# A two-layer gated-DeltaNet and sliding-window decoder trunk: the buffers, the places and the applied product of the adaLN modulation

## The chip, the cores and the metric

The kernel runs on one core of one Trainium2 chip. The metric is the device time of one execution in microseconds (us); of the kernel before, three runs have a median of 2365.28 us (2364.86 to 2368.85).

## The reference

All arithmetic is float32. Sequence length is 256, model width 2048, two layers. What matters here:

```python
c_act = silu(c)
for l in range(2):
    mod = c_act @ ada_w[l] + ada_b[l]                  # 2048 -> 3 x 2048
    shift, scale, gate = split(mod, 3)
    h = rmsnorm(x, norm_w[l]) * (1 + scale) + shift
    u = h @ w_in[l]                                    # q,k,v,beta,a,z_A | q,k,v,z_B | g_A,g_B
    o_a = gated_delta_rule(conv_silu(q, k, v), beta, a) -> per-head rmsnorm * silu(z_A)
    o_b = sliding_window_attention(rope(q), rope(k), v, sinks) * silu(z_B)
    y = sigmoid(g_A) * (o_a @ proj_a) + sigmoid(g_B) * (o_b @ proj_b)
    x = x + gate * (y @ w_out)
x = rmsnorm(x, final_norm_w)
```

`mod` is one vector of 6144 numbers per layer; its matrix `ada_w` holds 2048 x 6144 floats per layer and is read once.

## The kernel before, in words

**Layout.** Everything is kept transposed: features on the 128 partitions, the 256 tokens in the free dimension. A projection is cut into *tiles* of 128 output features. One tile needs a weight block of 128 x 2048 floats, which comes as two *halves* of 128 x 1024 (512 KB each).

**Products in two parts.** Each weight half is split into a high part and a remainder, so that TensorE's faster float32r products keep the precision: `load_half` (line 196) loads it into a buffer `win`, ScalarE casts it into `whi` (line 201) and VectorE subtracts to give `wlo` (line 202). The buffers are rings: five `win`, four `whi`, three `wlo` (line 31). The moving operand `h` is split the same way. `proj` (line 292) runs 16 k-steps per tile, each of two matmuls: `whi` with both parts of `h` (512 columns, line 289) and `wlo` with the high part (256 columns, line 290).

**Order of the work.** `_plan` (line 46) lists the tiles of a layer. Layer 0 begins with 32 gate tiles computed together while the modulation for layer 0 is made (`group_first`); layer 1 begins with a group of 8 (`group_next`). Then come, in both layers, `ba`, `kb`, `vb` (5 tiles); twice the batch `qa`, `ka`, `va` (8 tiles each) and `qb`/`zb` (16 tiles together); `za` (16); `pa` (16, in layer 1 with 8 gate tiles between); `pb` (16, in layer 1 with 16 gate tiles between); `wo` (16). The main loop (lines 965 to 999) takes them one by one: it loads the weights of the tile two ahead, emits the matmuls, advances the background work (the DeltaNet chain of a batch runs in pieces, one per tile, among the tiles that follow), calls the tile's handler, which evacuates the result, and may then emit modulation work. The tile framework turns this program order into one static order per engine; engines then wait for each other by semaphores, each one strictly in its order. All transfers are issued from SyncE's queue (SP), also in a fixed order.

**Background work of note.** `gdn_k` (line 589) inverts 32 x 32 triangles by 62 small VectorE operations (lines 644 to 653), sends the result through DRAM (`ydr`, `xdr`, lines 658 to 670) and TensorE then multiplies it (`T1p`, line 679). This falls into the `qb`/`zb` stage of each batch.

**Modulation.** The vectors for layer 0's shift and scale are made at the start (`ada_start`). The other 64 blocks (gate of layer 0; scale, shift, gate of layer 1) are made among the tiles: `ada_job` (line 171) makes one block of 128 values out of two halves of 128 x 1024. Each half is loaded into a buffer *of the weights' ring* (tag `win`, line 166) and at once multiplied and summed by one VectorE instruction (line 168); after the second, one or two tiny instructions (lines 177, 180) finish the block. A table `ADA_RATE` (line 28) says how many blocks each kind of tile is due; when the sum reaches one, a whole block, so two halves one behind the other, is emitted after the tile's handler (lines 991 to 994). By the start of `wo` in layer 0, 48 blocks must be there, and what is missing is emitted at once (line 977).

**The end of a layer.** `h_wo` (line 926) adds the gated product to x (lines 934, 935), squares it for the norm, and, in layer 0, writes the new x to DRAM (line 940), multiplies it *in place* by the next layer's scale (line 941) and makes the two float32r parts of the product (lines 949, 950) for the group of 8 gate tiles. `h_step` (line 376) later multiplies the scaled x by the row's reciprocal root to make `h`.

Of the kernel before, what the change touches and what calls it, by code (L numbers as in the profile page):

```python
# [11 lines left out]
F32 = mybir.dt.float32  # L12
F32R = mybir.dt.float32r
I32 = mybir.dt.int32
AF = mybir.ActivationFunctionType
ALU = mybir.AluOpType
# [3 lines left out]
P = 128  # L20
D = 2048
S = 256
KT = 16
# [1 line left out]
NH = 16  # L25
HB = 8
NB = NH // HB
ADA_RATE = [dict(qa=0.45, ka=0.45, va=0.0, qb=0.275, zb=0.275, za=0.54, pa=0.54, pb=0.54), dict(ga=0.3, pa=0.3, gb=0.3, pb=0.3)]
GRP = [32, 8]
SEG = [(0, 0, 4), (1, 0, 8), (0, 4, 12), (1, 8, 16), (0, 12, 16)]  # L30
NWIN, NWHI, NWLO = 5, 4, 3
BIG = 1.0e30
EPS = 1e-6

# [83 lines left out]
def build(nc):  # L118
# [11 lines left out]
    with ExitStack() as ctx:  # L130
# [3 lines left out]
        wp = pool("wp", 3)  # L134
        b8 = pool("b8", 1)
        sm = pool("sm", 2)
# [25 lines left out]

        modc = const.tile([P, L, 3, KT], F32, name="modc")

        def ada_half(l, part, ct, hf, acc):
            t = wp.tile([P, 1024], F32, name="adaw", tag="win", bufs=NWIN)
            dma(t, ada_d[l, part, ct, :, hf * 1024:(hf + 1) * 1024])
            V.scalar_tensor_tensor(t, t, 1.0, cact[:, hf * 1024:(hf + 1) * 1024], op0=ALU.mult, op1=ALU.mult,  # L168
                                   accum_out=acc[:, hf:hf + 1])

        def ada_job(l, part, ct):
            acc = sm.tile([P, 2], F32, name="modr", tag="modr", bufs=4)
            for hf in range(2):
                ada_half(l, part, ct, hf, acc)
            m = modc[:, l, part, ct:ct + 1]
            b = par[l][:, PC_ADAB + part * KT + ct:PC_ADAB + part * KT + ct + 1]
            V.tensor_scalar(m, acc[:, 0:1], acc[:, 1:2], b, op0=ALU.add, op1=ALU.add)
            if part == 1:
                nw = par[l][:, PC_NW + ct:PC_NW + ct + 1]
                V.tensor_scalar(m, m, 1.0, nw, op0=ALU.add, op1=ALU.mult)  # L180
# [194 lines left out]

        def h_step(l, k, xa, rstd, dst):
            t = sm.tile([P, S], F32, name="hn", tag="tA", bufs=3)
            V.tensor_tensor(t, xa, rstd, op=ALU.mult)
            sh = modc[:, l, 0, k:k + 1]
            A.activation(dst[:, 0:S], t, AF.Identity, bias=sh)  # L380
            V.scalar_tensor_tensor(dst[:, S:2 * S], t, sh, dst[:, 0:S].bitcast(F32), op0=ALU.add, op1=ALU.subtract)
# [39 lines left out]
        dma(par[1], par_d[1])  # L421
        rope_tables()
        ada_todo = [(0, 2, k) for k in range(KT)] + [(1, p_, k) for p_ in (1, 0, 2) for k in range(KT)]

        for l in range(L):
            pr = par[l]
# [499 lines left out]
            def h_wo(ps, i):  # L926
                nonlocal nacc, nlast
                if i % 8 == 0:
                    xnext[i // 8] = big("x", [P, 8, S], ("GT", "Y")[i // 8])
                xo = xnext[i // 8][:, i % 8, :]  # L930
                xr = sm.tile([P, S], F32, name="xr", tag="tB", bufs=2)
                dma(xr, x_d[i] if l == 0 else prev_x[i])
                gt = modc[:, l, 2, i:i + 1]
                V.scalar_tensor_tensor(xr, ps[:, S:2 * S], gt, xr, op0=ALU.mult, op1=ALU.add)
                V.scalar_tensor_tensor(xo, ps[:, 0:S], gt, xr, op0=ALU.mult, op1=ALU.add)
                if i == 0:
                    nacc = sm.tile([P, S], F32, name="nacc", tag="cv", bufs=2)
                nlast = norm_acc(nacc, xo, i)
                if l < L - 1:
                    dma(xs_dram[i], xo)  # L940
                    V.tensor_scalar(xo, xo, modc[:, l + 1, 1, i:i + 1], None, op0=ALU.mult)
                    n = S + 2
                    if i % 4 == 0:
                        raw.append(big("raw", [P, 4, 2 * n], ("QKT", "ek", "oT", "oT")[i // 4], F32R))
                        sh = modc[:, l + 1, 0, i:i + 4].unsqueeze(2).broadcast_to([P, 4, 2])
                        A.copy(raw[-1][:, :, S:n], sh)
                        V.tensor_tensor(raw[-1][:, :, n + S:2 * n], sh, raw[-1][:, :, S:n].bitcast(F32), op=ALU.subtract)
                    r = raw[-1][:, i % 4, :]
                    A.copy(r[:, 0:S], xo)
                    V.tensor_tensor(r[:, n:n + S], xo, r[:, 0:S].bitcast(F32), op=ALU.subtract)  # L950
                else:
                    V.tensor_scalar(xo, xo, pr[:, PC_FNW + i:PC_FNW + i + 1], None, op0=ALU.mult)

# [11 lines left out]
            for n in range(GRP[l], NT):  # L965
# [5 lines left out]
                for a in range(n, n + AHEAD + 1):  # L971
# [2 lines left out]
                            load_w(l, a)  # L974
                    elif l < L - 1 and (l + 1, a - NT) not in gtiles:
                        load_g(l + 1, a - NT)
                while what == "wo" and l == 0 and len(ada_todo) > KT:
                    ada_job(*ada_todo.pop(0))
                mov = {"pa": oA_hl, "pb": oB_hl, "wo": y_hl}.get(what, h)
                pg = proj(l, n, mov)  # L980
                ps = next(pg)
# [5 lines left out]
                if r is not None:  # L987
                    w = next(r, "end")
                    if w != "end":
                        streams.append([r, w or 0])  # L990
                acc_ada += ADA_RATE[l].get(what, 0.0)
                while ada_todo and acc_ada >= 1.0:
                    ada_job(*ada_todo.pop(0))
                    acc_ada -= 1.0
                if what == "za" and i % HB == HB - 1:
                    split_oA(i // HB)
# [85 lines left out]
```

## Time and profile before

| what | value |
|---|---|
| median of the three timed runs | 2365.28 us |
| the profiled execution, its own time | 2367.93 us |
| its span, first to last instruction | 2366.1 us |
| granted TensorE clock, mean | 0.989 |
| TensorE busy | 2292.6 us |
| VectorE busy | 1787.0 us |
| ScalarE busy | 1371.2 us |
| modulation instruction of line 168 | 128 times, 1221 ns in the mean |
| remainder of a weight half, line 202 | 724 times, 1220 ns in the mean |

In the rows of the profile PE is TensorE, PEld its weight loads, DVE is VectorE, ACT is ScalarE, SP is SyncE, which issues the transfers; `L202` is line 202 of the kernel. A row of the view by stretches gives, for a stretch of time in us from the start of the span: its length, then for each engine the busy time and in brackets the number of instructions, then the granted TensorE clock as a share of full speed, the share of the DMA engines' time in use, and GB/s. A row of the waits gives who waited for whom: the sum in us, how often, the longest. Matmuls overlap in the pipeline, so busy time of TensorE is not work at its peak.

### The profile page before, as it was taken

What the parts mean: (1) busy time and instruction counts of PE and PEld (TensorE: products, weight loads), DVE (VectorE), ACT (ScalarE), POOL (GpSimd) and SP (SyncE); (2) the same over time, 40 slices, a digit from 0 to 9 for tenths busy, and PEclk for the clock granted to TensorE, in tenths of its full rate; (3) what the DMA queues carried; (4) which work ended last, traced back from release to release, by engine and by line L of the source; (5) the groups of instructions that cost most, each with busy time, mean ns of one, the idle gap of its engine ahead of it and who ended that gap; (6) DMA issues with size and microseconds to landing.
All of it is one profiled execution on the core that took longest, in us unless ns stands there. A gap on an engine that the chain in (4) does not pass through costs nothing.

```text
span 2366.1 us, 39958 instructions
## 1 busy us (share of the span) xinstructions
PE 2292.6 (97%) x15094; PEld 2026.3 (86%) x15094; DVE 1787.0 (76%) x3160; ACT 1371.2 (58%) x2605; POOL 13.9 (1%) x20
## 2 busy tenths in 40 slices
PE   7999999899999998999999999999999999999997
PEld 6999888788887887888889888898888888888886
DVE  7997887866889677788676778757785567677766
ACT  4436556667666664444455665777667755444442
POOL 0000000000000000000000000000000000000000
PEclk9999999999999999999999999999999999999999
DMA  9998675656766567898766555635555467777764
GB/s 365 364 359 283 235 245 186 193 177 204 246 199 211 171 221 264 295 318 292 232 204 199 195 181 183 187 121 197 191 167 167 140 205 265 243 243 253 243 203 142
DMA packets 185603, 531.75 MB, mean 225 GB/s; under 512 B 40449, under 2 KB 69697, under 8 KB 179905
## 3 DMA queue, kind: packets, MB, share of 16 engines
q1 hardware_dynamic: 185410, 529.20, 66.9%
q8 instruction: 118, 1.93, 0.3%
q14 instruction: 75, 0.61, 0.1%
HBM read 512.26 MB, written 16.88 MB: 224 GB/s over the span
## 4 chain that ended last, share of the span: by engine, by line
PE 75%; DVE 11%; DMA 9%; issue 3%; ACT 2%; SPq 0%; DVEq 0%; ACTq 0%
PE mm L289 38%; PE mm L290 20%; DVE wlo L202 4%; DMA adaw<-ada 4%; PE mmg L251 2%; PE mmg L249 2%; PE mmg L250 2%; DMA xs_dram<-x 1%; DVE adaw L168 1%; DMA win<-w 1%; DMA oBs<-ob_dram 1%; PE o L742 1%; DVE cv L526 1%; PE sc L844 1%; PE ptr L871 1%
## 5 line engine op out<-in xcount | busy, mean ns | idle before, releaser
L289 PE MATMUL mm<-h,whi 128*128 128x512 f32 x3616 | 1292.3, 398 | 0.0
L202 DVE TENSOR_TENSOR wlo<-win,whi 128x1024 fp32r<-128x1024 f32 x724 | 882.0, 1220 | 244.7 <-PE mm L290 131.0
L290 PE MATMUL mm<-h,wlo 128*128 128x256 f32 x3616 | 1025.4, 284 | 7.1 <-DVE wlo L202 7.1
L201 ACT CAST whi<-win 128x1024 fp32r<-128x1024 f32 x724 | 753.4, 1047 | 443.1 <-PE mm L289 227.5
L289 PEld LDWEIGHTS mm<-h,whi 128*128 128x128 f32 x3616 | 681.7, 189 | 157.4 <-issue 4.3
L290 PEld LDWEIGHTS mm<-h,wlo 128*128 128x128 f32 x3616 | 682.7, 189 | 10.6 <-DVE wlo L202 10.2
L168 DVE SCALAR_TENSOR_TENSOR adaw<-adaw,cact 128x1024 f32<-128x1024 f32 x128 | 155.8, 1221 | 69.7 <-DMA adaw<-ada 69.4
L289 PE MATMUL mm<-oAhl,whi 128*128 128x512 f32 x512 | 184.4, 401 | 6.3 <-DVE oAhl L322 4.2
L289 PE MATMUL mm<-yhl,whi 128*128 128x512 f32 x512 | 181.8, 397 | 3.1 <-DVE yhl L924 3.1
L289 PE MATMUL mm<-oBhl,whi 128*128 128x512 f32 x512 | 180.8, 396 | 0.0
L317 DVE TENSOR_TENSOR ub<-ub,mm 128x256 f32<-128x256 f32 x290 | 120.7, 416 | 68.9 <-ACT ub L316 68.2
L526 DVE SCALAR_TENSOR_TENSOR cv<-ub,par,cv 128x255 f32<-128x255 f32 (+2 forms) x288 | 138.1, 480 | 32.6 <-ACT cv L524 29.1
L290 PE MATMUL mm<-oAhl,wlo 128*128 128x256 f32 x512 | 146.1, 286 | 1.1 <-DVE wlo L202 1.1
L290 PE MATMUL mm<-yhl,wlo 128*128 128x256 f32 x512 | 145.6, 284 | 1.6 <-DVE wlo L202 1.4
L249 PE MATMUL mmg<-h,whi 128*128 128x256 f32 x512 | 139.8, 287 | 6.3 <-ACT h L373 6.1
L290 PE MATMUL mm<-oBhl,wlo 128*128 128x256 f32 x512 | 144.2, 282 | 0.0
L250 PE MATMUL mmg<-h,whi 128*128 128x256 f32 x512 | 142.5, 286 | 0.0
L251 PE MATMUL mmg<-h,wlo 128*128 128x256 f32 x512 | 135.7, 287 | 3.2 <-DVE wlo L202 3.2
L316 ACT COPY ub<-mm 128x256 f32<-128x256 f32 x290 | 107.2, 370 | 38.0 <-PE mm L290 37.9
L289 PEld LDWEIGHTS mm<-oAhl,whi 128*128 128x128 f32 x512 | 98.1, 192 | 29.9 <-DVE oAhl L322 4.5
L289 PEld LDWEIGHTS mm<-yhl,whi 128*128 128x128 f32 x512 | 96.8, 189 | 25.8 <-DVE yhl L924 3.4
L289 PEld LDWEIGHTS mm<-oBhl,whi 128*128 128x128 f32 x512 | 96.2, 188 | 22.9
(261 smaller groups left out, 2600.2 us busy)
## 6 DMA issues: line engine op xcount, KB each, us to landing
win<-w SPq DMA_DIRECT2D x724, 512.0 KB, 4.7
adaw<-ada SPq DMA_DIRECT2D x128, 512.0 KB, 4.8
adab<-ada SPq DMA_DIRECT2D x31, 1024.0 KB, 8.7
sg<-sig_dram SPq DMA_DIRECT2D x40, 128.0 KB, 5.6
sig_dram<-gacc SPq DMA_DIRECT2D x4, 1024.0 KB, 5.5
E<-gc_dram SPq DMA_DIRECT2D x4, 1024.0 KB, 8.4
GT<-GT_d SPq DMA_DIRECT2D x4, 1024.0 KB
ob_dram<-zbs SPq DMA_DIRECT2D x32, 128.0 KB, 3.9
```

Source lines behind the costliest of these rows:

```text
L168: V.scalar_tensor_tensor(t, t, 1.0, cact[:, hf * 1024:(hf + 1) * 1024], op0=ALU.mult, op1=ALU.mult, accum_out=acc[:, hf:hf + 1])
L201: A.copy(h, w)
L202: V.tensor_tensor(o, w, h.bitcast(F32), op=ALU.subtract)
L249: T.matmul(d, hi, m[:, 0:S], start=(k == b0 and t % 2 == 0), stop=False)
L250: T.matmul(d, hi, m[:, S:2 * S], start=False, stop=False)
L251: T.matmul(d, lo, m[:, 0:S], start=False, stop=(k == b1 - 1 and t % 2 == 1))
L289: T.matmul(ps[:, :], hi[k // 8][:, c0:c0 + P], m, start=(k == 0), stop=False)
L290: T.matmul(ps[:, S:2 * S], lo[k // 8][:, c0:c0 + P], m[:, 0:S], start=False, stop=(k == KT - 1))
L316: A.copy(t, ps[:, S:2 * S])
L317: V.tensor_tensor(t, t, ps[:, 0:S], op=ALU.add)
L526: V.scalar_tensor_tensor(y[:, j:], u[:, :S - j], w(3 - j), y[:, j:], op0=ALU.mult, op1=ALU.add)
L742: T.matmul(p[:, i - h0, :], lhs, rhs, start=(j == 0), stop=(j == len(ops) - 1))
```

## The change

Five edits, in the diff below:

- **Buffer.** A half of the modulation matrix no longer takes a slot of the weights' ring; it has one buffer of its own (tag `adaw`, one buffer of the same size), and the weights' ring has four slots instead of five.
- **Load and step parted.** `ada_load` only issues the transfer, `ada_step` only multiplies and sums. At the top of each tile of layer 0 (and of `ga`, `pa`, `gb`, `pb` of layer 1), behind the weights' loads, the next half is loaded if none is waiting; it is consumed at the end of that tile or a later one.
- **Unit.** The unit of the schedule is a half, no longer a block of two; with one buffer, at most one half is consumed per tile.
- **Rates.** `ADA_RATE` of layer 0 is spread over all kinds of tiles (in blocks per tile): fewer in `qa`, `ka`, some in `va`, more in `qb`, `zb`, a little more in `za`, fewer in `pa`, `pb`.
- **x.** The new x is not scaled in place: line 941 goes; the scale is an operand of ScalarE's cast (now an activation with a scale) and of VectorE's remainder, and `h_step` multiplies by scale and root in one instruction, as `h_step0` already does.

```diff
-ADA_RATE = [dict(qa=0.45, ka=0.45, va=0.0, qb=0.275, zb=0.275, za=0.54, pa=0.54, pb=0.54), dict(ga=0.3, pa=0.3, gb=0.3, pb=0.3)]
+ADA_RATE = [dict(qa=0.25, ka=0.25, va=0.15, qb=0.45, zb=0.45, za=0.6, pa=0.45, pb=0.45), dict(ga=0.3, pa=0.3, gb=0.3, pb=0.3)]
-NWIN, NWHI, NWLO = 5, 4, 3
+NWIN, NWHI, NWLO = 4, 4, 3
...
-        def ada_half(l, part, ct, hf, acc):
-            t = wp.tile([P, 1024], F32, name="adaw", tag="win", bufs=NWIN)
+        ada_acc = {}
+        ada_in = []
+
+        def ada_load():
+            l, part, ct, hf = ada_todo.pop(0)
+            t = wp.tile([P, 1024], F32, name="adaw", tag="adaw", bufs=1)
             dma(t, ada_d[l, part, ct, :, hf * 1024:(hf + 1) * 1024])
+            ada_in.append((l, part, ct, hf, t))
+
+        def ada_step():
+            l, part, ct, hf, t = ada_in.pop(0)
+            if hf == 0:
+                ada_acc[l, part, ct] = sm.tile([P, 2], F32, name="modr", tag="modr", bufs=4)
+            acc = ada_acc[l, part, ct]
             V.scalar_tensor_tensor(t, t, 1.0, cact[:, hf * 1024:(hf + 1) * 1024], op0=ALU.mult, op1=ALU.mult,
                                    accum_out=acc[:, hf:hf + 1])
-
-        def ada_job(l, part, ct):
-            acc = sm.tile([P, 2], F32, name="modr", tag="modr", bufs=4)
-            for hf in range(2):
-                ada_half(l, part, ct, hf, acc)
+            if hf == 0:
+                return
...
         def h_step(l, k, xa, rstd, dst):
             t = sm.tile([P, S], F32, name="hn", tag="tA", bufs=3)
-            V.tensor_tensor(t, xa, rstd, op=ALU.mult)
+            V.scalar_tensor_tensor(t, xa, modc[:, l, 1, k:k + 1], rstd, op0=ALU.mult, op1=ALU.mult)
...
+        ada_todo = [(*job, hf) for job in ada_todo for hf in range(2)]
...
-                    V.tensor_scalar(xo, xo, modc[:, l + 1, 1, i:i + 1], None, op0=ALU.mult)
...
-                    A.copy(r[:, 0:S], xo)
-                    V.tensor_tensor(r[:, n:n + S], xo, r[:, 0:S].bitcast(F32), op=ALU.subtract)
+                    sc = modc[:, l + 1, 1, i:i + 1]
+                    A.activation(r[:, 0:S], xo, AF.Identity, scale=sc)
+                    V.scalar_tensor_tensor(r[:, n:n + S], xo, sc, r[:, 0:S].bitcast(F32), op0=ALU.mult, op1=ALU.subtract)
...
-                while what == "wo" and l == 0 and len(ada_todo) > KT:
-                    ada_job(*ada_todo.pop(0))
+                while ada_todo and len(ada_in) < 1 and (l == 0 or what in ("ga", "pa", "gb", "pb")):
+                    ada_load()
+                while what == "wo" and l == 0 and len(ada_todo) + len(ada_in) > 2 * KT:
+                    ada_step()
+                    ada_load()
...
-                acc_ada += ADA_RATE[l].get(what, 0.0)
-                while ada_todo and acc_ada >= 1.0:
-                    ada_job(*ada_todo.pop(0))
+                acc_ada += 2 * ADA_RATE[l].get(what, 0.0)
+                while ada_in and acc_ada >= 1.0:
+                    ada_step()
                     acc_ada -= 1.0
```

## The prediction

> **What bounds the kernel now.** I read the page first, then the stretches of the two layers beside each other, then TensorE's waits. From the page:
>
> ```profile
> span 2366.1 us, 39958 instructions
> PE 2292.6 (97%) x15094; PEld 2026.3 (86%) x15094; DVE 1787.0 (76%) x3160; ACT 1371.2 (58%) x2605; POOL 13.9 (1%) x20
> PE 75%; DVE 11%; DMA 9%; issue 3%; ACT 2%; SPq 0%; DVEq 0%; ACTq 0%
> ```
>
> TensorE is the bound, yet a quarter of the chain that ended last is not TensorE's. Where that is, two tables by stage show. The stages of layer 0, in order: `qa`-`ka`-`va` of batch 0, `qb`/`zb` of batch 0, the same two of batch 1, `za`, `pa`+`pb`, `wo`. Columns: length, then busy time and (count) of PE, PEld, DVE, ACT, POOL, then granted clock, DMA share, GB/s.
>
> ```profile
> 247.60:402.00 154.40, 149.27 (x883) 131.35 (x881) 127.53 (x220) 96.03 (x214) 1.10 (x2) 0.99 0.68 226
> 402.00:535.40 133.40, 125.44 (x1036) 108.41 (x1034) 98.81 (x238) 85.20 (x175) 0.52 (x1) 0.97 0.59 187
> 535.40:697.60 162.20, 156.36 (x959) 137.81 (x955) 128.43 (x234) 110.28 (x275) 2.91 (x3) 1.00 0.64 213
> 697.60:826.30 128.70, 124.29 (x1035) 107.69 (x1033) 98.36 (x238) 85.54 (x175) 0.52 (x1) 0.99 0.62 199
> 826.30:929.00 102.70, 99.18 (x594) 86.70 (x591) 78.07 (x135) 61.38 (x131) 0.00 (x0) 1.00 0.72 238
> 929.00:1121.60 192.60, 185.21 (x1026) 160.51 (x1025) 156.71 (x248) 85.30 (x118) 0.00 (x0) 0.97 0.87 298
> 1121.60:1220.10 98.50, 93.58 (x514) 79.58 (x512) 68.84 (x118) 45.85 (x69) 0.00 (x0) 0.98 0.71 229
> ```
>
> The same stages of layer 1, where the sixth holds 56 tiles (24 gate tiles more):
>
> ```profile
> 1301.70:1449.50 147.80, 147.28 (x882) 130.38 (x881) 113.12 (x185) 95.84 (x213) 1.09 (x2) 1.00 0.57 186
> 1449.50:1571.50 122.00, 121.95 (x1036) 106.42 (x1034) 88.55 (x216) 85.37 (x175) 0.52 (x1) 1.00 0.55 171
> 1571.50:1726.70 155.20, 155.20 (x958) 137.91 (x955) 115.65 (x199) 110.75 (x275) 2.92 (x3) 1.00 0.54 175
> 1726.70:1849.00 122.30, 122.08 (x1035) 106.42 (x1034) 86.52 (x208) 85.58 (x175) 0.52 (x1) 1.00 0.54 167
> 1849.00:1947.40 98.40, 98.40 (x594) 86.74 (x591) 60.83 (x88) 63.54 (x132) 0.00 (x0) 1.00 0.54 176
> 1947.40:2262.80 315.40, 315.19 (x1795) 275.32 (x1794) 222.69 (x310) 153.19 (x214) 0.00 (x0) 1.00 0.74 246
> 2262.80:2353.00 90.20, 90.20 (x515) 78.89 (x514) 60.38 (x93) 38.58 (x48) 0.00 (x0) 1.00 0.54 172
> ```
>
> The matmul counts agree, so layer 1 is a measured copy of layer 0 without modulation (with less of it in the sixth stage), and there TensorE does not pause. A tile of its sixth stage takes 315.40/56 = 5.63 us. Layer 0 takes longer by 6.6, 11.4, 7.0, 6.4, 4.3, 192.6 - 32 x 5.63 = 12.4, and 8.3 us: **56.4 us**, 48.1 of them ahead of `wo`. That is all that the change can gain in these stages. TensorE's waits, first in layer 0 from `qa` to the start of `wo`, then in layer 1:
>
> ```profile
> PE mm L290 <- DVE wlo L202: 8.0, 8, 1.5
> PE T1p L679 <- DMA mt<-xdr: 5.6, 1, 5.6
> PE sst L533 <- ACT qT L527: 4.3, 3, 1.9
> PE GT_t L452 <- DVE brk L596: 4.2, 2, 2.7
> PE mm L289 <- DVE oAhl L322: 4.2, 1, 4.2
> PE mm L289 <- DVE yhl L924: 3.1, 1, 3.1
> ```
>
> ```profile
> PE sst L533 <- ACT qT L527: 0.5, 1, 0.5
> PE mm L290 <- DVE wlo L202: 0.2, 1, 0.2
> ```
>
> VectorE stands behind nearly all of them, itself or by way of ScalarE or a transfer: it is late. What makes it late is the modulation, in the same stretch of layer 0:
>
> ```profile
> L168 DVE SCALAR_TENSOR_TENSOR adaw<-adaw,cact x98: 1209/1220/1228, 266.4 to 1128.1; 128x1024 f32<-128x1024 f32 x98
> L168 DVE DVE_READ_ACCUMULATOR adaw<-adaw,cact x98: 74/82/86, 267.6 to 1129.2; 128x1 f32 x98
>   DMA adaw<-ada: 44.6, 31
> DMA to landing us min/median/max: 3.5/4.8/7.3
> ```
>
> 98 halves take 1.22 + 0.08 = 1.30 us each, and VectorE stood 44.6 us waiting for their transfers: 0.46 per half, 1.76 together, and two come in a row.
>
> **The change part by part.** *Rates.* Halves due, before (rate x tiles x 2): 14.4, 8.8, 14.4, 8.8, 17.3, 34.6 for the six stages ahead of `wo` (98.3; the row says 98). After: 10.4, 14.4, 10.4, 14.4, 16 and 32; `za` is due 19.2, but one buffer allows one per tile, and the backlog fills `pa` and `pb`. So VectorE does the same work (97), less of it in `qa`-`va`, and 5.6 halves more in each `qb`/`zb`.
>
> *Load a tile ahead.* I take the wait at 0.2 us per half, between none and the 0.46 of today, nearer to none since most halves now have a tile's 5.63 us for a landing of 4.8. A half then costs 1.5 us: 15.6, 21.6, 15.6, 21.6, 24 and 48 us by stage, against 25.3, 15.5, 25.3, 15.5, 30.4 and 60.9 before. If the loss went with VectorE's time in each stage, it would be 4.1, 16.0, 4.4, 8.9, 3.4 and 9.8: 46.6 instead of 48.1, no gain. The gain must come from breaking the pairs: a pair blocks VectorE for 2 x 1.76 = 3.5 us, a single one for 1.5. For `qa`-`va`, `za` and `pa`+`pb`, where VectorE is idle 17 to 24% of the time (127.53 of 154.40 busy, 78.07 of 102.70), I take half of the proportional loss (2.0, 2.2, 1.7, 4.9); the ends are zero, as in layer 1, and the whole. For `qb`/`zb` I take 0.85 of it, 21.2 us, since there the inversion fills VectorE for tiles on end and the amount counts: that is 3.4 us worse than today's 17.8.
>
> *One buffer.* In `za`, `pa`, `pb` step, load and landing form a loop of 1.30 + 4.8 = 6.1 us by the median landing, against 5.63 per tile. From 800 to 900 us, mostly `za`, the landings are shorter:
>
> ```profile
> DMA to landing us min/median/max: 3.7/4.3/6.2
> ```
>
> 1.30 + 4.3 = 5.6 just fits. I put 2 us down for it. The waiting load stands in SP's fixed order; behind it wait the next tile's two weight halves, `sg` rows in `pa` and `pb`, and the chain's DRAM transfers in `qb`/`zb`. The Trainium skill, *DMA: Bandwidth & Descriptors*, section on the anatomy of a DMA, fits a transfer (on GpSimd's path) by 2.0 us and the bytes over 436 GB/s. By that, a half lands in 3.2 us as an estimate, the loop is 4.5 and the 2 us fall away; no landing in the trace is below 3.5, so I keep them.
>
> So the six stages lose 2.0 + 2.2 + 1.7 + 4.9 + 21.2 + 2 = 34.0 instead of 48.1: **14.1 gained**.
>
> A stall costs more than its wait. Two short stretches of `pa`:
>
> ```profile
> 936.00:948.00 12.00, 8.53 (x40) 7.43 (x41) 9.83 (x14) 4.36 (x6) 0.00 (x0) 0.86 0.64 216
> 960.00:982.00 22.00, 18.77 (x92) 15.76 (x91) 17.26 (x27) 8.99 (x12) 0.00 (x0) 0.84 0.85 291
> ```
>
> TensorE idles 3.5 and 3.2 us there and the granted clock falls to 0.86 and 0.84 besides. My sum uses lengths of stages, which hold both. The Trainium skill, *TensorE: Matmul & The Clock Gate*, part 1, has the clock halved only after an idle window of about 3.4 us; by that, ending a wait of under 3 us saves the wait alone. The six stages' idle time, 34.3 us of the 48.1, would then shrink to 34.3/48.1 of my gain, 10.1 instead of 14.1. The second stretch, with 3.2 us of idle time in all, speaks against it.
>
> *x not scaled in place.* In `wo` of layer 0, and in the group behind it:
>
> ```profile
> L949 ACT CAST raw<-x 128x256 fp32r<-128x256 f32 x15 | 6.1, 407 | 30.4 <-DVE x L941 30.4
> L950 DVE TENSOR_TENSOR raw<-x,raw 128x256 fp32r<-128x256 f32 x14 | 5.9, 419 | 0.0
> L941 DVE TENSOR_SCALAR x<-x,modc 128x256 f32<-128x256 f32 x15 | 5.3, 354 | 26.5 <-DMA xs_dram<-x 26.5
> ```
>
> ```profile
> L381 DVE SCALAR_TENSOR_TENSOR h<-hn,modc,h 128x256 fp32r<-128x256 f32 x16 | 7.1, 478 | 0.0
> ```
>
> Line 941 waits until x has been written out, 26.5 us of VectorE, and goes with its 354 ns; the remainder becomes the form of 478 ns instead of 419, so VectorE saves 0.3 us per tile and the waits. Nothing is late behind it but the weights' remainders. `h_step` grows by about 0.06 us x 16, beside TensorE's group. Two stretches of `wo`, an early and a later one:
>
> ```profile
> 1135.00:1157.00 22.00, 22.00 (x126) 19.27 (x126) 14.71 (x24) 11.41 (x16) 0.00 (x0) 1.00 0.70 221
> 1157.00:1218.00 61.00, 59.51 (x332) 50.56 (x331) 41.76 (x70) 27.24 (x40) 0.00 (x0) 1.00 0.69 215
> ```
>
> At the pace of the first, the second's 332 matmuls would take 332 x 22.00/126 = 58.0 us: 3.0 of the 8.3 us that `wo` loses are these waits, the rest lies where `pb` hands over (`yhl`, 3.1 above), to a VectorE that halves in pairs, two of them at the start of `wo`, keep late. I take **6 gained**, ends 3 and 8.3.
>
> *Ring of four.* SP waits for the ring today, and the first 200 us run near full transfer load:
>
> ```profile
> SPq L198 <- DVE wlo L202: 1043.8, 458, 7.6
> ```
>
> ```profile
> 60.00:160.00 100.00, 97.76 (x816) 97.36 (x815) 93.01 (x110) 42.16 (x50) 0.00 (x0) 1.00 0.93 355
> ```
>
> Each half's load starts half a tile, 2.8 us, later. Four slots in two tiles leave 11.3 us for a landing (4.8), cast and remainder (1.22), so later stages hide it; at the start I put **1 lost**, ends 0 and 8.
>
> Sum: 14.1 + 6 - 1 = 19.1. The profiled execution took 2367.93 us, its span 2366.1; 2367.9 - 19.1 = 2348.8. The median of the runs, 2365.28, is 2.65 lower: **2346**.
>
> **The rivals.** *The single buffer paces `za`, `pa`, `pb`* (slower). If a landing takes 5.2 us there, since each load queues behind two weight halves, the loop is 6.5 against 5.63: 0.87 x 48 tiles, less one tile of lead, 36 us in place of my 8.6: 2374. It cancels the whole gain from 5.0 on. For: the median of 4.8. Against: the 4.3 of `za`, and that half of the present landings are second in a pair.
>
> *The inversion is crowded.* Each of the 11.2 halves added to `qb`/`zb` pushes the chain behind `T1p` by its full 1.30: 17.8 + 14.6 = 32.4 instead of 21.2, so 2357. For: the 5.6 us wait at `T1p`. Against: pairs are gone there too.
>
> *All comes back.* Layer 0 runs nearly like layer 1: losses of 12 instead of 34, `wo` 8.3, no loss at the start: 2321. For: layer 1's sixth stage holds 0.3 blocks per tile and loses nothing.
>
> *The waits stay* because the fixed order places the steps too early as today: 1.76 per half, 48 lost, only `wo` gains: 2360. *The ring of four starves the start*: 8 us lost, 2353.
>
> **How the numbers follow.** Forecast 0.48, with a range of its own of 2336 to 2356; single buffer 0.15; crowded inversion 0.12; all back 0.13; waits stay 0.07; ring 0.05. 0.2% is 4.7 us, about what a measurement of this kernel can tell. Faster by more than that, below 2360.6: forecast, all back, ring, and most of the crowded case, 0.75; slower: the single buffer beyond its 5.0, 0.12; the same 0.13. The range from 2322 to 2370 leaves out the outer part of the all-back case and of the single buffer, about 0.1 on each side.
>
> **What would show it.** Right: the waits of VectorE on `adaw` fall from 44.6 us in layer 0 to below 20; `qa`-`va` and `pa`+`pb` come within 3 and 8 us of layer 1's; no wait on `xs_dram` by VectorE and `wo` near 92 us; `qb`/`zb` as long as before or longer, still with a wait at `T1p`. Wrong: SP waiting for the modulation step for more than 100 us and tiles of `pb` above 5.7 us (single buffer), or layer 1's stages longer than shown above (ring).

## The result: 34 us slower, and the profile after

The changed kernel takes 2399.36 us (median of four runs, 2395.23 to 2400.91) against 2365.07 us of the kernel before (four runs, 2360.65 to 2368.85): a ratio of 1.0125, 95% interval 1.0108 to 1.0142. The forecast was 2346. The profiled execution took 2398.06 us, its span is 2396.3 us, 30.2 longer than before. From the page of the changed kernel: span, busy time of the engines, the chain that ended last.

```profile
span 2396.3 us, 39962 instructions
PE 2301.6 (96%) x15094; PEld 2029.4 (85%) x15094; DVE 1791.6 (75%) x3144; ACT 1372.5 (57%) x2607; POOL 14.0 (1%) x20
PE 65%; DMA 18%; DVE 13%; issue 4%; ACT 1%; SPq 0%; DVEq 0%; ACTq 0%
```

The engines do what they did before, to within 9 us. But TensorE's part of the chain falls from 75% to 65%, and transfers' doubles, from 9% to 18%. Where that is, the stages of layer 0 show, in the order of the prediction's first table: `qa`-`ka`-`va` and `qb`/`zb` of batch 0, the same of batch 1, `za`, `pa`+`pb`, `wo`. The eighth row is the group of 8 gate tiles behind them.

```profile
247.00:405.70 158.70, 150.77 (x889) 131.89 (x887) 137.48 (x250) 98.47 (x217) 1.10 (x2) 0.99 0.75 247
405.70:541.90 136.20, 126.79 (x1036) 109.64 (x1033) 105.00 (x252) 85.89 (x176) 0.51 (x1) 0.96 0.65 205
541.90:706.70 164.80, 158.23 (x956) 138.93 (x955) 141.91 (x267) 109.68 (x274) 2.92 (x3) 0.99 0.73 239
706.70:843.50 136.80, 126.39 (x1036) 108.88 (x1033) 104.72 (x249) 85.47 (x176) 0.51 (x1) 0.97 0.66 207
843.50:954.10 110.60, 103.03 (x590) 88.41 (x590) 79.61 (x133) 60.57 (x131) 0.00 (x0) 0.98 0.71 233
954.10:1157.20 203.10, 186.24 (x1027) 158.27 (x1025) 151.83 (x234) 84.23 (x118) 0.00 (x0) 0.99 0.82 270
1157.20:1255.80 98.60, 93.68 (x517) 81.06 (x515) 75.25 (x120) 47.96 (x72) 0.00 (x0) 0.97 0.79 249
1255.80:1303.00 47.20, 47.20 (x388) 46.82 (x387) 35.28 (x56) 26.27 (x37) 1.81 (x1) 1.00 0.56 181
```

Against before the first seven rows are 4.3, 2.8, 2.6, 8.1, 7.9, 10.5 and 0.1 us longer, 36.3 together; the group is 5.0 shorter. Its row in the kernel before:

```profile
1220.10:1272.30 52.20, 48.73 (x389) 48.30 (x390) 37.99 (x65) 28.46 (x41) 1.82 (x1) 0.97 0.54 179
```

VectorE is busier in the first four rows (137.48 us against 127.53 in the first, for one), so it does more there, not only waits more. In layer 1 only the sixth stage has changed, and not in its length. Its row in the changed kernel:

```profile
1978.10:2292.90 314.80, 314.80 (x1794) 275.38 (x1793) 190.07 (x235) 153.88 (x214) 0.00 (x0) 1.00 0.60 196
```

It was 315.40 us before, with VectorE busy 222.69 us in 310 instructions; now 190.07 in 235. The modulation has left it. The view of the modulation's tile says where it went, first the kernel before, then the changed one. In the first row of each, the last figures before the shapes are the first and last start; the second row is VectorE's wait for the halves' transfers (us, times), and the third has a digit for each fortieth of the span, the share of it that these instructions fill, in tenths.

```profile
L168 DVE SCALAR_TENSOR_TENSOR adaw<-adaw,cact x128: 1209/1220/1228, 266.4 to 2235.3; 128x1024 f32<-128x1024 f32 x128
  DMA adaw<-ada: 69.4, 53
busy tenths in 40 slices 0000110001100012222000000000000001111100
```

```profile
L179 DVE SCALAR_TENSOR_TENSOR adaw<-adaw,cact x128: 1205/1225/1227, 224.3 to 1196.9; 128x1024 f32<-128x1024 f32 x128
  DMA adaw<-ada: 132.8, 91
busy tenths in 40 slices 0000121111111121122100000000000000000000
```

Before, 98 halves lay in layer 0 and 30 in layer 1, in clusters that follow the table of rates. Now all 128 lie in layer 0, in every stage of it (2 in `ba` to `vb`, then 22, 13, 24, 14, 18, 29 and 6 in the seven stages of the table), from the second tile behind the start on: the 30 that the program places in `ga` to `pb` of layer 1 are done before layer 1 begins. And VectorE waits for their transfers 132.8 us, 91 times, instead of 69.4 us. How such a wait arises, a stretch of `pb` shows: first VectorE's rows of the modulation (start, duration, and in brackets the wait before), then SP's issues.

```profile
1117.24 1.23 DVE L179 SCALAR_TENSOR_TENSOR adaw<-adaw,cact 128x1024 f32<-128x1024 f32 x1 [1.67 <-DMA adaw<-ada]
1123.95 1.23 DVE L179 SCALAR_TENSOR_TENSOR adaw<-adaw,cact 128x1024 f32<-128x1024 f32 x1 [1.65 <-DMA adaw<-ada]
1130.11 1.23 DVE L179 SCALAR_TENSOR_TENSOR adaw<-adaw,cact 128x1024 f32<-128x1024 f32 x1 [0.72 <-DMA adaw<-ada]
```

```profile
1118.51 0.33 SPq L171 DMA_DIRECT2D adaw<-ada  x1
1119.98 0.33 SPq L206 DMA_DIRECT2D win<-w  x1
1120.74 0.33 SPq L917 DMA_DIRECT2D sg<-sig_dram  x1
1122.37 0.33 SPq L206 DMA_DIRECT2D win<-w  x1
1125.22 0.33 SPq L171 DMA_DIRECT2D adaw<-ada  x1
```

A step begins at 1117.24 us; its buffer is free at 1118.5 and the next load goes out at 1118.51; it lands, and the next step begins, at 1123.95; the next load goes out at 1125.22. Step and load follow each other without a pause, with periods of 6.7 and 6.2 us, and each time VectorE stands 0.7 to 1.7 us with the tile's remainders (`wlo`) queued behind. TensorE feels it there, from `qa` to the end of `wo`:

```profile
PE mm L298 <- DVE wlo L210: 30.3, 32, 2.6
PE sc L853 <- DVE zbs L891: 8.9, 2, 5.9
PE GT_t L461 <- DVE brk L605: 7.6, 2, 4.5
PE T1p L688 <- DMA mt<-xdr: 7.3, 2, 6.0
PE mm L297 <- DVE yhl L933: 3.9, 1, 3.9
```

The wait for `wlo` was 9.4 us, 12 times, in the same stretch before (the prediction's 8.0 us end at 1135 us).

### The profile page after: what moved, and what is told of

The parts are those of the page before. It is cut to its first block, busy times and chain, and to the rows that moved or that the text cites. A ratio compares the mean times of both kernels' runs of the same rounds, so it can differ in the third digit from the quotient of the medians.

```text
span 2396.3 us, 39962 instructions
## 1 busy us (share of the span) xinstructions
PE 2301.6 (96%) x15094; PEld 2029.4 (85%) x15094; DVE 1791.6 (75%) x3144; ACT 1372.5 (57%) x2607; POOL 14.0 (1%) x20
## 4 chain that ended last, share of the span: by engine, by line
PE 65%; DMA 18%; DVE 13%; issue 4%; ACT 1%; SPq 0%; DVEq 0%; ACTq 0%
PE mm L297 33%; PE mm L298 17%; DMA adaw<-ada 14%; DVE wlo L210 4%; DVE adaw L179 3%; PE mmg L259 2%; PE mmg L258 2%; PE mmg L257 2%; DMA sg<-sig_dram 1%; DMA win<-w 1%; PE mmg L281 1%; DMA oBs<-ob_dram 1%; DVE adab L194 1%; PE mmg L282 1%; PE mmg L283 1%
## 5 line engine op out<-in xcount | busy, mean ns | idle before, releaser
L298 PEld LDWEIGHTS mm<-h,wlo 128*128 128x128 f32 x3616 | 684.6, 189 | 21.6 <-DVE wlo L210 20.9
L179 DVE SCALAR_TENSOR_TENSOR adaw<-adaw,cact 128x1024 f32<-128x1024 f32 x128 | 156.5, 1223 | 133.0 <-DMA adaw<-ada 132.8
L298 PE MATMUL mm<-oBhl,wlo 128*128 128x256 f32 x512 | 145.1, 283 | 9.6 <-DVE wlo L210 9.6
```

The costliest lines, as they stand in the source:

```text
L298: T.matmul(ps[:, S:2 * S], lo[k // 8][:, c0:c0 + P], m[:, 0:S], start=False, stop=(k == KT - 1))
```

## The experiments

**The theories.** *F (freed):* in the kernel before, a half takes its slot from the weights' ring, whose slots are given out in program order, and so its step stays at its tile. With a buffer of its own nothing but that buffer ties the step; the static order places it as early as its load allows, whatever the table says, and the real landing comes later than that place. *P, the rival,* keeps to the frame of the prediction: the steps stand where the new table puts them, and their places and the pace of the one buffer make the loss. Twelve kernels were run, each timed against the kernel before in the same sitting; all figures by stage are from their profiles. In the expectations, `after` is the changed kernel.

### One part alone, and one part undone

`x_only`: the kernel before with only the last of the five edits, x not scaled in place.

```diff
-                    V.tensor_scalar(xo, xo, modc[:, l + 1, 1, i:i + 1], None, op0=ALU.mult)
...
-                    A.copy(r[:, 0:S], xo)
+                    A.activation(r[:, 0:S], xo, AF.Identity, scale=sc)
...
```

> The kernel before with one edit alone: the new x is not scaled in place. Theory F (the own buffer lets the modulation run free; the x edit is good by itself) expects no wait of VectorE on xs_dram, 3 us less in wo and up to 5 us less in the group of 8 gate tiles behind it (that group took 52.2 us before and 47.2 after): 2355 to 2362. If the group's 5 us came instead from the modulation being finished early, only wo shrinks: 2361 to 2364.

Measured: 2357.18 us, ratio 0.9963 (0.9946 to 0.9979), 10.05 us below the kernel before of that sitting (2367.23); span 2351.7. `wo` is 94.7 us instead of 98.5, the group 47.2 instead of 52.2: this part alone gains. (The other 5.6 of the 14.4 us between the two profiled spans lie in stages that the edit does not touch; single executions of the kernel before range from 2363.07 to 2374.91 us in that sitting.) The two rows are `wo` and the group.

```profile
1116.50:1211.20 94.70, 90.93 (x517) 79.05 (x515) 71.11 (x111) 49.63 (x75) 0.00 (x0) 1.00 0.79 247
1211.20:1258.40 47.20, 47.20 (x389) 46.82 (x388) 35.24 (x56) 26.28 (x37) 1.82 (x1) 1.00 0.57 182
```

`old_rates`: the changed kernel with the table of before.

```diff
-ADA_RATE = [dict(qa=0.25, ka=0.25, va=0.15, qb=0.45, zb=0.45, za=0.6, pa=0.45, pb=0.45), ...
+ADA_RATE = [dict(qa=0.45, ka=0.45, va=0.0, qb=0.275, zb=0.275, za=0.54, pa=0.54, pb=0.54), ...
```

> The kernel after with the table of rates of before, so fewer modulation halves due in qb/zb and none in va. Theory F: the table no longer decides anything, the steps go where the planner finds VectorE free and the half landed, so the time stays at 2395 to 2402 and all 128 steps still lie in layer 0. Theory P (the halves that the table adds to qb/zb, and the loop of the one buffer in za, pa and pb, cost the time): qb/zb come back by some 15 us in all, 2375 to 2388.

Measured: 2395.97 us, ratio 1.0145 (1.0111 to 1.0178), span 2388.5, again 128 halves in layer 0, 124.2 us of waits, and every stage within 3.4 us of the changed kernel's, `qb`/`zb` within 2: the 15 us that P expected back there did not come. A table that decides nothing cannot have been wrong: the part of P that rests on it falls.

`held`: the changed kernel, but the factor 1.0 of the step is a column that ScalarE makes out of the current tile's product (0 times the product plus one), so that a step cannot stand ahead of its tile.

```diff
+            one = sm.tile([P, 1], F32, name="one", tag="one", bufs=4)
+            A.activation(one, ps[:, 0:1], AF.Identity, bias=ones[:, 0:1], scale=0.0)
-            V.scalar_tensor_tensor(t, t, 1.0, cact[:, hf * 1024:(hf + 1) * 1024], op0=ALU.mult, op1=ALU.mult,
+            V.scalar_tensor_tensor(t, t, one, cact[:, hf * 1024:(hf + 1) * 1024], op0=ALU.mult, op1=ALU.mult,
...
```

> The kernel after with one addition: the modulation instruction takes its factor 1.0 from a one-column tile that ScalarE writes from the current tile's PSUM (128 instructions more on ScalarE), so that a step cannot stand ahead of the tile that emits it. Theory F: 97 or 98 steps in layer 0 and the rest in layer 1, VectorE's waits on the halves fall from 132.8 us to below 60, time 2340 to 2365. Theory P: the one buffer still paces za, pa and pb, where one half per tile is due, and tiles there take 6.2 us or more: 2375 to 2400. Theory R (the ring of four): no change, 2395 to 2400.

Measured: 2366.34 us, ratio 0.9985 (0.9971 to 1.0), span 2367.7: 28.6 us of the 30.2 are back by this one tie, although it adds 128 instructions to ScalarE. The time is 1.3 us above F's range; theory R, the ring of four, expected no change and falls. 97 halves lie in layer 0, as the table has it. VectorE waits 52.7 us for halves (132.8 in the changed kernel) and 13.3 us for ScalarE's column. The first six stages of `held`:

```profile
248.10:395.20 147.10, 147.10 (x881) 130.28 (x879) 123.05 (x208) 96.72 (x222) 1.11 (x2) 1.00 0.67 218
395.20:527.40 132.20, 126.11 (x1035) 108.60 (x1033) 105.81 (x253) 88.20 (x190) 0.52 (x1) 0.97 0.68 213
527.40:683.00 155.60, 155.50 (x959) 137.99 (x955) 125.85 (x225) 111.44 (x283) 2.93 (x3) 1.00 0.65 212
683.00:816.70 133.70, 126.81 (x1035) 108.92 (x1033) 104.51 (x252) 88.78 (x191) 0.52 (x1) 0.97 0.65 206
816.70:918.70 102.00, 99.42 (x594) 86.66 (x591) 74.55 (x127) 64.11 (x145) 0.00 (x0) 1.00 0.71 236
918.70:1127.80 209.10, 189.91 (x1026) 158.88 (x1025) 158.86 (x243) 90.91 (x149) 0.00 (x0) 0.98 0.80 269
```

`qa`-`va` are as long as in layer 1, to 0.7 us: there the change does all that was hoped for. But `pa`+`pb` are 209.1 us, 16.5 more than before. The chain inside that stretch of `held` is mostly the loop of the one buffer, 62.6% loads of halves and 8.9% their steps:

```profile
by line: DMA adaw<-ada 62.6%; DVE adaw L181 8.9%; issue 8.8%; DMA win<-w 7.5%; PE mm L299 5.6%; PE mm L300 2.8%; DVE wlo L212 2.0%; DVE oBhl L332 1.1%; ACT whi L211 1.0%; DVE oAhl L332 0.6%; DVE ub L327 0.6%; ACT oAhl L331 0.5%; ACT oBhl L3
```

So F is the main cause of the slowdown. When the steps are held, the design still gains nothing, because `pa` and `pb` take back what the other stages gain, and there the chain runs through P's loop.

`ring_half`: the changed kernel with its halves back in slots of the weights' ring of five.

```diff
-NWIN, NWHI, NWLO = 4, 4, 3
+NWIN, NWHI, NWLO = 5, 4, 3
...
-            t = wp.tile([P, 1024], F32, name="adaw", tag="adaw", bufs=1)
+            t = wp.tile([P, 1024], F32, name="adaw", tag="win", bufs=NWIN)
```

> The kernel after, but the modulation half again takes a slot of the weights' ring, which has five slots: the unit of a half, the load at the top of the tile, the new rates and the x edit stay. Theory F: the ring hands out its slots in the order of the program and so holds the steps to their tiles: 98 steps in layer 0, waits below 60 us, time 2340 to 2362. If instead the new rates or the single halves are what costs, it stays above 2375.

Measured: 2368.77 us, ratio 1.0006 (0.9994 to 1.0019), span 2363.7, above the 2340 to 2362 expected. The ring too keeps the steps in their places: 98 halves in layer 0, and 52.4 us of waits on them. Layer 0 from `qa` to `wo` takes 959.8 us (972.5 before, 1008.8 in the changed kernel), but `ga` to `pb` of layer 1 grow by 15.2 us, with 88.1 us of waits on halves there. All waits on halves, 140.6 us, are more than the changed kernel's 132.8, and the time is 30.6 us less: the sum of VectorE's waits alone does not give the time.

### More buffers, held and free; another table; smaller loads

To take no more space in SBUF, the on-chip memory of the buffers, a second buffer for halves is bought with a slot of the weights' ring (three instead of four).

```diff
-NWIN, NWHI, NWLO = 4, 4, 3
+NWIN, NWHI, NWLO = 3, 4, 3
...
-            t = wp.tile([P, 1024], F32, name="adaw", tag="adaw", bufs=1)
+            t = wp.tile([P, 1024], F32, name="adaw", tag="adaw", bufs=2)
...
-                while ada_todo and len(ada_in) < 1 and (l == 0 or what in ("ga", "pa", "gb", "pb")):
+                while ada_todo and len(ada_in) < 2 and (l == 0 or what in ("ga", "pa", "gb", "pb")):
```

`held_two` is `held` with this, `free_two` the changed kernel with this.

> The steps held to their tiles, with two buffers for halves (up to two loaded ahead) and a weights' ring of three to make room. Theory F (freed steps are the main cause) with a loop of the one buffer second: the loop is gone, pa and pb together fall from the 209.1 us of held to 185-195, VectorE's waits on halves from 67.9 us to below 15, qa-va stay at 147 and 155, the span comes to 2345-2358. Rival P2 (pa and pb are long because each step takes VectorE's time and load bandwidth at one per tile, buffers or not): pa and pb stay above 203, the span stays within 6 us of 2367.7. Rival R (a ring of three starves the products): layer 1's stages without modulation, the same to 0.3 us in all kernels so far, grow, and the start too.

Measured: 2410.79 us, ratio 1.0172 (1.0152 to 1.0193), span 2412.5. VectorE waits only 1.1 us for halves now; the other 22.1 us in front of its steps are waits for ScalarE's column. `pa`+`pb` fall to 200.4, 8.7 us less than in `held` and still 20.2 above the pace of layer 1, so the theory's 185 to 195 was too hopeful: either the loop was not all that was lost there, or the ring of three costs there too; this run cannot part them. What sinks the kernel is the ring of three (rival R): the start takes 235.0 us instead of 217.9, `ba` to `vb` 34.4 instead of 30.2, and `ga` to `pb` of layer 1 332.1 instead of 314.8, some 39 us in all, where going from five to four had cost nothing. The last of the three needs the halves beside the small ring: `free_two`, which has no halves there, keeps its 315.0 us. The sixth stage of layer 1 in `held_two`:

```profile
1975.70:2307.80 332.10, 321.26 (x1794) 275.17 (x1793) 224.51 (x313) 159.02 (x245) 0.00 (x0) 1.00 0.70 231
```

> The changed kernel as it is, steps not held, with two buffers for halves and a weights' ring of three. If what costs is VectorE standing in front of halves that have not landed (133 us of waits in after), the waits fall below 60 us and the time to 2365-2385. If what costs is the place of the steps (all 128 in layer 0, some 30 us more of VectorE's own work there, in front of other work), the waits fall as well but the time stays at 2390-2405, with the steps ending earlier than at 1197 us. If the steps remain tied to landings (each load issued at a step's end), they come in pairs at about half the period, 128 of them before some 850 us, and the stages behind run like layer 1's.

Measured: 2399.09 us, ratio 1.0129 (1.011 to 1.0147), span 2395.4, the steps from 215.3 to 925.0 us, waits on halves 38.1 us. The time alone would speak for the second reading, and would mislead: by stages, the ring of three takes 20.5 us at the start (238.9 against 218.4), 6.7 in `ba` to `vb` and 4.6 in layer 1; without these, layer 0 from `qa` to `wo` is 976.2 us, 32.6 less than in the changed kernel, though 121 halves are done in it, nearly as many as there (126). So it is not the 30 halves more in layer 0 by themselves that cost 36 us. How much of the 32.6 is the waits, and how much comes from `pa` and `pb` holding no halves any more (180.5 us here), this run cannot part: from `qa` to `qb`/`zb` it takes 5.2 us more than the changed kernel, with 33 halves more and 32.7 us of waits less.

`held_rates` is `held` with another table for layer 0.

```diff
-ADA_RATE = [dict(qa=0.25, ka=0.25, va=0.15, qb=0.45, zb=0.45, za=0.6, pa=0.45, pb=0.45), ...
+ADA_RATE = [dict(qa=0.4, ka=0.4, va=0.25, qb=0.35, zb=0.35, za=0.47, pa=0.4, pb=0.4), ...
```

> held with another table for layer 0: qa, ka 0.4, va 0.25, qb, zb 0.35, za 0.47, pa, pb 0.4, about as many halves in all. If the one buffer's loop of some 6.5 us paces pa and pb of held only because a step is due in nearly every tile there, 0.8 per tile leaves room: pa and pb 190-198 in place of 209.1, qb and zb together 5-8 us shorter than held's 265.9, while qa, ka, va rise by 0-6 us; span 2345-2357. If a step costs the same wherever it lies, the span stays within 5 us of 2367.7.

Measured: 2353.23 us, ratio 0.9931 (0.9914 to 0.9949), span 2351.6. `pa`+`pb` 198.7 (0.7 above the range), both `qb`/`zb` 259.2 (6.7 less), `qa` to `va` 7.5 longer (1.5 above the range). Where a step is held to its tile the table matters; where it is free, `old_rates` had shown, it does not.

`held_quarter` is `held` with quarters of 128x512 in two buffers, the same space; `free_quarter` the changed kernel with them.

```diff
-            t = wp.tile([P, 1024], F32, name="adaw", tag="adaw", bufs=1)
-            dma(t, ada_d[l, part, ct, :, hf * 1024:(hf + 1) * 1024])
+            t = wp.tile([P, 512], F32, name="adaw", tag="adaw", bufs=2)
+            dma(t, ada_d[l, part, ct, :, hf * 512:(hf + 1) * 512])
...
```

> held with quarters of 128x512 in place of halves, in two buffers of the same 4 KB in all: twice as many steps of about half the length, two loads in the air. If the loop of one buffer (landing, then step, then the next load) is what pa and pb of held lose, they fall from 209.1 us to 188-198 and VectorE's waits from 67.9 us to below 30; span 2342-2357. If the number of steps and their fixed cost count (twice as many waits, sums and one-column products, about 0.3 us each), qa-va rise by 3-8 us and the span stays at 2360-2375.

Measured: 2358.67 us, ratio 0.9957 (0.9942 to 0.9972), span 2356.1: inside the first range, but not for its reason. VectorE's waits for the loads fall from 52.7 us to 27.8 (those for ScalarE's column rise from 13.3 to 20.0), and yet `pa`+`pb` stay at 208.7; the gain on `held` is in `wo` (93.7 instead of 99.2) and `qb`/`zb` (262.6 instead of 265.9). The chain in `pa`+`pb` has changed hands, from the modulation's loads to the weights':

```profile
by line: DMA win<-w 37.3%; DMA adaw<-ada 17.6%; issue 11.5%; DVE wlo L213 7.6%; DVE adaw L181 5.6%; ACT whi L212 5.4%; DVE ub L328 2.3%; PE mm L300 1.7%; PE mm L301 1.0%; SPq L920 0.9%; DVE yhl L936 0.7%; DVE ub L933 0.7%; DVE modc L188 0.7
```

and SP stands there 69.8 us, 31 times, in front of a modulation load whose buffer is not free, with the weights' loads behind it:

```profile
SPq L171 <- DVE adaw L181: 69.8, 31, 6.4
```

> The changed kernel, ring of four, steps not held, with quarters of 128x512 in two buffers of the same 4 KB in place of halves in one. Theory F2 (what costs in after is a freed step that meets an unlanded load, not the 30 halves more in layer 0): two loads in the air cut VectorE's waits from 133.0 us to 40-80 and layer 0 from qa to wo, 1008.9 us in after and 976.1 in free_two, to 970-990; layer 1 stays as in after; span 2357-2378. Rival C (the place of the steps costs: 128 of them in front of layer 0's other work): layer 0 stays above 1000 us, the span above 2387, whatever the waits do.

Measured: 2416.63 us, ratio 1.0201 (1.0179 to 1.0224), span 2415.7. The waits hardly fell (123.9 us, 101 times), so the run does not part F2 from C as it was meant to. Layer 0 from `qa` to `wo` is 1028.4 us, 19.6 longer than in the changed kernel; the 256 steps take VectorE 198 us (0.691 + 0.083 each) where the 128 took 167. With two loads in the air the steps stand closer together (3.6 us from one to the next in the mean, (1153.6 - 223.5)/255), and still in front of their landings.

### The ring once more, and the table moved on

`ring_l0` is `ring_half` with the load a tile ahead in layer 0 alone.

```diff
-                while ada_todo and len(ada_in) < 1 and (l == 0 or what in ("ga", "pa", "gb", "pb")):
+                while ada_todo and len(ada_in) < 1 and l == 0:
...
-                while ada_in and acc_ada >= 1.0:
+                while (ada_in or ada_todo) and acc_ada >= 1.0:
+                    if not ada_in:
+                        ada_load()
```

> ring_half (a half in a slot of the weights' ring of five, which keeps the steps in their places), but loaded a tile ahead in layer 0 alone; in layer 1 the load stands at its step, as in the kernel before. If ring_half lost its 15.2 us of layer 1's ga/pa and gb/pb because a slot was held for the tiles between a load and its step, these two come back to 135-136 and 179-180 us and the span to 2345-2352; layer 0 stays at its 959.7 us from qa to wo within 4. If they were lost to the order of the loads as such, the span stays within 5 us of 2363.7.

Measured: 2380.67 us, ratio 1.0052 (1.0035 to 1.0068), span 2375.6. Layer 1's `ga` to `pb` stay at 332.3 us: the reason given, a slot held from load to step, falls. The stretch has the same 30 halves as before, but VectorE waits 90.3 us for them instead of 24.8. First `ring_l0`, then the kernel before:

```profile
  DMA adaw<-ada: 90.3, 28
DMA to landing us min/median/max: 5.4/5.6/6.2
```

```profile
  DMA adaw<-ada: 24.8, 22
DMA to landing us min/median/max: 4.7/4.7/4.9
```

The visible difference is that before, two halves are loaded and stepped together, and here one at a time. VectorE comes to its step 2.5 us after the load was issued, in the mean, and before 4.3 us after it; why, stays open. Layer 0 came out 10.8 us longer than in `ring_half`, outside the 4 expected. Its text is not quite the same: the new loop lets `za`, where 1.2 halves are due per tile, load and take a second half in one tile, so 17 lie in `za` and 29 in `pa`+`pb` instead of 14 and 32. But 6.1 of the 10.8 us arise ahead of `za`, where the work of VectorE, ScalarE and SP stands in the same order in both kernels; these have no explanation here, and differences of this size between other pairs of these kernels need not come from the edit either.

`ring_l0_rates` is `ring_l0` with the table of `held_rates`.

> ring_l0 with the table of held_rates (qa, ka 0.4, va 0.25, qb, zb 0.35, za 0.47, pa, pb 0.4 in layer 0). In held this table took 10.4 us off pa and pb and 6.8 off both qb/zb and gave some of it back in qa to va, 15.3 us off layer 0. If the loop of the one buffer was the reason, less is to be had here, where pa and pb are 194.0 already: 187-193, qb/zb 124-128 each, qa to va 4-8 us longer, span 2340-2350, at most 6 us below ring_l0. If it is the load on VectorE and on the transfers at one half per tile, the gain is as large as in held: 12-16 us below ring_l0.

Measured: 2388.94 us, ratio 1.0086 (1.0064 to 1.0108), span 2387.6, 12.0 longer than `ring_l0`: both readings expected a gain. `pa`+`pb` get 2.5 us shorter, `qa` to `va` grow by 9.8, with waits of 86.7 us in layer 0 instead of 75.5. A table found with one kind of buffer does not carry over to another.

`held_rates2` moves the table of `held_rates` on.

```diff
-ADA_RATE = [dict(qa=0.4, ka=0.4, va=0.25, qb=0.35, zb=0.35, za=0.47, pa=0.4, pb=0.4), ...
+ADA_RATE = [dict(qa=0.45, ka=0.45, va=0.3, qb=0.3, zb=0.3, za=0.5, pa=0.36, pb=0.36), ...
```

> held_rates with the table moved on the same way: qa, ka 0.45, va 0.3, qb, zb 0.3, za 0.5, pa, pb 0.36 in layer 0. By the difference of held and held_rates, a half more in qa to va costs about 0.7 us, a half less in qb/zb gives 1.4 and in pa and pb 2.0: some 7 more in qa to va (+5), 5 fewer in qb/zb (-7), 4 fewer in pa and pb (-8), 2 more in za (+1): 9 us below held_rates' span of 2351.6, 2339-2348. If at 0.9 halves per tile the loop of the one buffer (6.5 us against tiles of 5.9) begins to pace qa and ka as it paced pa and pb of held, these four lose 6-12 us and the span stays at 2349-2356.

Measured: 2349.25 us, ratio 0.992 (0.9893 to 0.9948), span 2348.3, the lowest of all, though its interval and that of `held_rates` overlap, at the edge between the two ranges. `pa`+`pb` fall by 8.0 us as expected; `qa` and `ka` of both batches together grow by 4.4, and both `qb`/`zb` by 2.3 where 7 less were expected. Its `pa`+`pb`:

```profile
923.00:1113.70 190.70, 183.61 (x1026) 158.70 (x1025) 149.92 (x225) 89.37 (x141) 0.00 (x0) 0.98 0.84 277
```

## Why the prediction was wrong, point by point

**The step that failed first: "VectorE does the same work (97)".** The prediction counted halves by the table. Freed of the weights' ring, the steps no longer obeyed it: 128 instead of 97 lay in layer 0, and `old_rates` showed the table to be without effect. It counted 10.4, 14.4, 10.4, 14.4, 16 and 32 for the six stages; 22, 13, 24, 14, 18 and 29 lay there. The terms for these six stages all rested on that count. The rival *the waits stay because the fixed order places the steps too early* named the nearest mechanism, with the wrong price: it kept 98 halves and 1.76 us each. A half took 1.22 + 0.08 + 132.8/128 = 2.34 us of VectorE, 300 us in layer 0 where the prediction had 97 x 1.5 = 146.

**"Load a tile ahead", wait at 0.2 us per half.** It was 1.04. There is no tile of lead when the step moves up to its load. Of the signs set for being right, only the missing wait on `xs_dram` and the longer `qb`/`zb` with their wait at `T1p` appeared; `qa`-`va` lie 10.9 and 9.6 us above layer 1's, and `pa`+`pb` 22.9. Held to the tile, the lead appears, in `qa`-`va` at least: no wait on halves there in `held`, and losses against layer 1 of -0.7 and 0.4 us where the prediction put 2.0 and 2.2.

**`qb`/`zb`, 21.2 us lost.** In the changed kernel 28.7. Held, 132.20 + 133.70 - 122.0 - 122.3 = 21.6, which fits the number, but by luck as far as the runs show: the reason given was that the amount of VectorE's work counts there, and `ring_half`, with the same 14 and 15 halves, loses 12.5 (126.1 and 130.7 us).

**One buffer, 2 us.** The second step that failed, by the size. It took a landing of 4.3 us from a row of 800 to 900 us; that row is the view of the weights' halves (`win`), not of the modulation's. For the modulation's own halves in `pa` and `pb` of the kernel before, the same view says 6.0 us in the median, from the three loads whose landing it records there:

```profile
DMA to landing us min/median/max: 4.8/6.0/6.1
```

In `held`, the 22 halves of `pa` and `pb` for which VectorE waited took 5.1 us from issue to step in the median (4.4 to 7.1), so the loop is 6.5 us against 5.63 per tile. `za` loses 3.6 and `pa`+`pb` 28.9 us against layer 1, 32.5 in all, where the prediction had 8.6 and its rival *the single buffer* 36, from a landing of 5.2 and the same loop of 6.5. For held steps the rival, which got 0.15, was near. Not all of the 28.9 need be the loop: the first two tiles of `pa` take 20.0 us instead of 11.3, with TensorE waiting 5.6 us for `oAhl`, and `held_two` got back only 8.7. By the fit of the Trainium skill, *DMA: Bandwidth & Descriptors*, section on the anatomy of a DMA (on GpSimd's path), a half would land in 3.2 us, as an estimate. No landing recorded for a half of the modulation in the changed kernel is as short, the median is 4.7. (The prediction's "no landing in the trace is below 3.5" holds for these halves alone: of the weights' halves in the group of the kernel before, some take 3.1.)

```profile
DMA to landing us min/median/max: 3.5/4.7/7.7
```

Holding the steps gives `held` 10.1 us in the first four stages; `za` to `pb` give back 15.8, and the 5.0 of the group leave it where the kernel before was. The tests set for this rival, SP waiting for the step for over 100 us and tiles of `pb` above 5.7, came true in the changed kernel (145.1 us, and tiles of 5.6 to 7.4, 6.4 in the mean), but they do not part it from F.

```profile
SPq L171 <- DVE adaw L179: 145.1, 57, 5.9
```

**x not scaled in place, 6 us.** Right in sign and cause, too small: `x_only` gains 3.8 us in `wo` and 5.0 in the group behind it, which the prediction did not price: before, TensorE waited 3.2 us for the last sum for the norm there, and the granted clock was 0.97; in the changed kernel it waits for nothing in that stretch, at 1.00. The kernel before:

```profile
PE nps L363 <- DVE nacc L358: 3.2, 1, 3.2
```

In the changed kernel `wo` is 98.6 us all the same, most likely since six halves with 7.1 us of waits stand in it; where none does, in `free_two`, `wo` is 90.4.

**Ring of four, 1 us.** Nothing: the start takes 218.4 us instead of 218.2, layer 1's stages are unchanged. One slot less again costs 17 us and more at the start.

**A stall costs more than its wait.** Borne out. In the first six stages the changed kernel loses 84.3 us against layer 1; TensorE is idle 58.8 of them. In the other 25.5 it is busy longer with the same matmuls; the granted clock of these rows (0.96 to 0.99, in layer 1 1.00), taken times their lengths, accounts for about 17 of them, as an estimate. The other price that the prediction weighed, by which ending a wait of under 3 us saves the wait alone, does not hold here: within its second stretch of `pa` the granted clock is 0.50 from 971.3 to 978.1 us, and TensorE's longest pause in the 8 us before that is 2.15 us.

## What to carry to other kernels

In a framework that makes the order itself, a shared ring of buffers is also a tie to the program's order: before giving a background task a buffer of its own, ask what will then keep it at its place, and if nothing does, add a dependency on the work that it should follow. A task with one buffer has a period of its landing plus its step, and the landing has to be taken under the load of the stage where it will run, not the best one. And judge a trade by stages: `free_two` had the time of the changed kernel, with two quite different losses in it.

## What had not been expected of the hardware and its order

A ring of weights of five or four slots makes no difference, one of three costs 17.1 us in the first 218 us (`held_two`) and 17.3 us in `ga` to `pb` of layer 1 where halves are loaded too, while `free_two`, with the same ring and no halves there, keeps 315.0 us: in that stretch the slot is missed only where the two kinds of loads meet. Halving the size of the loads and doubling their number left the length of `pa`+`pb` where it was (209.1 and 208.7 us), at 269 and 272 GB/s.
